# Filter chunks of a Hyena branch: one bank per parity of taps, wider steps, later matmuls, and another share for GpSimd

## The chip, the cores and the metric

The kernel runs on one core of a Trainium2 chip. The metric is device time in microseconds (us); of three runs the median counts. Engines are named as in the profile: PE (TensorE matmul), PEld (its weight loads), DVE (VectorE), ACT (ScalarE), POOL (GpSimd), SP (the queue that issues the DMAs).

## The reference

Two layers of an encoder trunk on x of 256 rows by 1024 columns, float32. Per layer:

```python
u = rms_norm(x, norm_mix_pre)
proj = u @ w_in                      # q, k, v of 3 groups x 4 heads, and hv, hx1, hx2
o_att = attention of the 3 dilated windows, mixed by their softmax denominators
filt = implicit_filters(...)         # a small MLP with sines -> 4 x 1024 channels x 256 taps, times a decay
z = hx1 * bidir_fft_conv(hv, filt[0], filt[1], hy_bias[0])
z = hx2 * bidir_fft_conv(z, filt[2], filt[3], hy_bias[1])
merged = sigmoid(u @ w_gate + b_gate) halves times (o_att @ w_o_attn, z @ w_o_hyena), summed
x = x + rms_norm(merged @ w_out, norm_mix_post)
x = x + rms_norm(swiglu(rms_norm(x, norm_ffn_pre)), norm_ffn_post)
```

The filters of a layer depend on its weights alone, not on x.

## The kernel before

**Precision.** Every big product is three matmuls (`mm3`): each float32 operand is split into a high and a low part, and high by high, high by low and low by high are summed. So each piece of weights (`raw`, 128 by 1024 or 128 by 768) is loaded by SP (L140), copied to `whi` by ACT (L86), and `wlo = raw - whi` is made by DVE or by POOL (L89). `split_lo` counts the pieces; each one whose count is a multiple of `POOL_LO` = 5 goes to POOL. A piece is split up to three pieces ahead of its use (`AHEAD`), and four raw buffers are in flight.

**Order of the work.** PE runs in the order in which the program writes its matmuls. The other engines' queues are put in order by a planner that simulates the program beforehand; the queues are then fixed and each engine works through its own strictly in order.

**Ticks.** Between two pieces of weights PE does a step of side work. Side jobs are Python generators in a queue; at most two are active; one `tick()` advances each active one to its next `yield`. So a `yield` more is a piece of weights (12 matmuls of 384 columns or 24 of 256) between two steps of a job. The jobs of the first layer's mixer, in queue order: two filter MLPs, constants, eight filter chunks (4 column groups `cc` times 2 convolutions `v`), attention slots 0 and 1, four jobs of two convolutions each (`both`), attention slots 2 and 3. Numbered from the mixer's start, the pieces are: slot 0 (pieces 1 to 4), slot 1 (5 to 16), the input columns of the Hyena branch (17 to 40), gates (41 to 56), slot 2 (57 to 68), slot 3 (69 to 80), the Hyena output projection (81 to 88). There is a tick after each. Before slot 3's values (piece 77) the program runs ticks until all four convolution jobs have ended, and then splits their result (`z_split`: `zh` on ACT, `zl` on DVE), which pieces 81 to 88 use.

**A filter chunk** (`filter_chunk`, one per `cc` and `v`) has three steps. *Load*: SP loads `w`, `dec` and `bb` (the bias row; one buffer only), POOL makes `sd` (sum and difference), ACT and DVE (POOL in layer 2) split it into `sh` and `sl`. *D*, two ticks later (four for the chunks with `cc == 2` of layer 2): for each parity `e` of taps two matmuls give `h`, DVE multiplies it by the decay in two 256-column instructions (`dd`, L315), ACT and DVE split it (`dh`, `dl`). *Z*, two ticks later: for each half `s` (cosine, sine) one PSUM bank takes both parities, 12 matmuls in all; then per `s` one 256-column `ev` (L332 on DVE, L334 on ACT) and two 256-column DVE instructions into the tables `K` (L337 to L341). Layer 1's eight chunks run in its mixer. Layer 2's first four run during layer 1's feed-forward part and its last four in layer 2's own mixer.

**Convolution and attention.** `conv` multiplies a transformed block `zz` by `K` (L562 to L564 on DVE, L565 and L566 on POOL). `attend` makes scores and a softmax (`S`, L634 to L639), yields three times, transposes the result on PE (L647, `PT`) and multiplies it by the values.

Of the kernel before, what the change touches and what calls it, by code (L numbers as in the profile page):

```python
# [44 lines left out]
def trunk(tc, nc, a, out):  # L45
# [4 lines left out]
    with es:  # L50
# [11 lines left out]
        def bigt(dt=F32, name="big"):  # L62
            return big.tile([P, 1024], dt, tag="big", bufs=22, name=name)
# [7 lines left out]
        def f256(name, dt=F32):  # L71
            return sm.tile([P, L], dt, tag="f256", bufs=4, name=name)
# [7 lines left out]
        def mm3(o, lh, ll, rh, rl, start, stop):  # L80
            mm(o, lh, rh, start, False)
            mm(o, lh, rl, False, False)
            mm(o, ll, rh, False, stop)
# [46 lines left out]

        source = order()
        loaded, halfway, ready = deque(), deque(), deque()
        shared = [True]
        count = [0, 0]

        def load(spare=False):
# [21 lines left out]
        def split_lo(eng=None):  # L158

            if halfway:  # L160
                raw, n, h, lo, own = halfway.popleft()
                count[1] += 1
                share = shared[0] and count[1] % POOL_LO == 0 or count[1] == 6
                lo_of(lo[:, :n], raw[:, :n], h[:, :n], nc.gpsimd if share else eng)
                ready.append((h, lo, own))

# [115 lines left out]
        def filter_chunk(l, v, cc, K, fd, shared):  # L282
            w = t512("w3")
            nc.sync.dma_start(w, a["w3"][l, v, cc])
            if v == 0:
                dec = sm.tile([P, 2, 256], F32, tag="dec", bufs=2, name="dec")
                nc.sync.dma_start(dec, a["dec"][cc])
                shared[cc] = dec
            dec = shared[cc]
            bb = sm.tile([P, 256], F32, tag="bb", bufs=1, name="bb")  # L290
            nc.sync.dma_start(bb, a["hyb"][l, v, cc * 256:(cc + 1) * 256].partition_broadcast(P))
            if cc % 2 == 0:
                for j in range(2):
                    K[v][j][cc // 2] = bigt(name=f"K{v}{j}{cc // 2}")
            sd = t512("sd")
            h = ptt(sd[:, 0:256], w[:, 0:256], w[:, 256:512], op=OP.add)
            late = l == 1 and cc == 2
            if late and v == 0:
                tc.keep_in_program_order(h)
            ptt(sd[:, 256:512], w[:, 0:256], w[:, 256:512], op=OP.subtract)  # L300
            sh, sl = r512("sh"), r512("sl")
            h = hi_of(sh, sd)
            if l == 0 and cc == 0:
                tc.keep_in_program_order(h)
            lo_of(sl, sd, sh, nc.gpsimd if l else None)
            for _ in range(4 if late else 2):
                yield
            Dh, Dl = [], []
            for e in range(2):
                h = acc()  # L310
                mm(h, gst[l][:, e, :], sh, True, False)
                mm(h, gst[l][:, e, :], sl, False, True)
                d = t512("dd")
                for q in range(2):
                    vtt(d[:, q * 256:(q + 1) * 256], h[:, q * 256:(q + 1) * 256], dec[:, e, :], op=OP.mult)  # L315
                dh, dl = r512("dh"), r512("dl")
                hi_of(dh, d)
                lo_of(dl, d, dh)
                Dh.append(dh)
                Dl.append(dl)  # L320
            yield
            yield
            hh, cq = cc // 2, cc % 2
            for s in range(2):
                z = acc()
                for e in range(2):
                    b = (2 * s + e) * P
                    mm3(z[:, e * 256:(e + 1) * 256], fd[:, b:b + P], fd[:, 512 + b:512 + b + P],
                        Dh[e][:, s * 256:(s + 1) * 256], Dl[e][:, s * 256:(s + 1) * 256], True, True)
                ev = f256("ev")  # L330
                if s == 0:
                    vtt(ev, z[:, 0:256], bb, op=OP.add)  # L332
                else:
                    nc.scalar.activation(ev, z[:, 0:256], AF.Copy)  # L334
                k0 = K[v][0][hh][:, cq * 512 + s * 256: cq * 512 + s * 256 + 256]
                k1 = K[v][1][hh][:, cq * 512 + s * 256: cq * 512 + s * 256 + 256]
                vtt(k0, z[:, 256:512], ev, op=OP.add)  # L337
                if s == 0:
                    vtt(k1, ev, z[:, 256:512], op=OP.subtract)
                else:  # L340
                    vtt(k1, z[:, 256:512], ev, op=OP.subtract)  # L341
            yield


# [193 lines left out]
        def conv(v, cc, z, xg, K):  # L538

            f, b = fold(z)  # L540
            eo = sm.tile([P, 2, 2, P], F32, tag="t512", bufs=7, name="eo")
            ptt(eo[:, 0].rearrange("p c (r a) -> p c r a", r=4), f, b, op=OP.add)
            ptt(eo[:, 1].rearrange("p c (r a) -> p c r a", r=4), f, b, op=OP.subtract)
            yield
            yield
            t = acc()
            for q in range(4):
                nc.tensor.transpose(t[:, q * P:(q + 1) * P], eo[:, q // 2, q % 2, :], ident)  # L548
            nh, nl = r512("nh"), r512("nl")
            hi_of(nh, t)  # L550
            lo_of(nl, t, nh)
            yield
            yield
            Y = []
            for j in range(2):
                zz = acc()
                for s in range(2):
                    mm3(zz[:, s * 256:(s + 1) * 256], dft_h[:, 2 * s + j, :], dft_l[:, 2 * s + j, :],
                        nh[:, s * 256:(s + 1) * 256], nl[:, s * 256:(s + 1) * 256], True, True)
                Kt = K[v][j][cc // 2][:, (cc % 2) * 512:(cc % 2) * 512 + 512]  # L560
                t1, t2 = t512("t1"), t512("t2")
                vtt(t1, zz, Kt, op=OP.mult)  # L562
                vtt(t2[:, 0:256], zz[:, 0:256], Kt[:, 256:512], op=OP.mult)
                vtt(t2[:, 256:512], zz[:, 256:512], Kt[:, 0:256], op=OP.mult)  # L564
                ptt(t1[:, 0:256], t1[:, 0:256], t1[:, 256:512], op=OP.subtract)  # L565
                ptt(t1[:, 256:512], t2[:, 0:256], t2[:, 256:512], op=OP.add)  # L566
                Y.append(t1)
            yield
            yield
            pq = acc()  # L570
            for c in range(2):
                for s in range(2):
                    w = slice(s * 256 + c * P, s * 256 + (c + 1) * P)
                    for j in range(2):
                        mm(pq[:, w], Y[j][:, w], inv[:, 2 * s + j, :], j == 0, j == 1)
            pe = f256("pe")
            nc.scalar.activation(pe, pq[:, 0:256], AF.Copy)
            ys = t512("ys")
            vtt(ys[:, 0:256], pq[:, 256:512], pe, op=OP.add)
            vtt(ys[:, 256:512], pe, pq[:, 256:512], op=OP.subtract)  # L580
            f, b = fold(xg)
            for q, w in enumerate((f, b)):
                ptt(w, w, ys[:, q * 256:(q + 1) * 256].rearrange("p (c r a) -> p c r a", c=2, r=4), op=OP.mult)
            yield
            yield
# [23 lines left out]
        def attend(s, qk, vt, OT):  # L609
# [16 lines left out]
            for i in range(2):  # L626
# [10 lines left out]
                nc.scalar.activation(Si, Si, AF.Exp, bias=nm, scale=SCALE, accum_out=den)  # L637
                nc.vector.reciprocal(rd, den)
                nc.vector.tensor_scalar(Si, Si, rd, None, op0=OP.mult)  # L639
            yield  # L640
            yield
            yield
            PT = bigt(name="PT")
            for i in range(2):
                t = acc()
# [27 lines left out]
        def mixer(l, U, o, K):  # L673
# [6 lines left out]
            def slot(s, qk, then=None):  # L680
                vt = bigt(name="vt")
                for j in range(3) if s else (2,):
                    if j == 2 and then:
                        while convs[0]:
                            tick()
                        then()
                    o = [acc() for i in range(2)]
                    for kk in range(4):
                        pc = piece()
                        for i in range(2):  # L690
                            rows_of(U, o[i], i, pc, kk, 384)
                        done(pc)
                        if kk < 3:
                            tick()
                    for i in range(2):
                        qkv_out(j, i, o[i], qk, vt)
                    tick()
                return attend(s, qk, vt, OT)

            queue.append(slot(0, qk))  # L700
            queue.append(slot(1, [bigt(name="qk") for i in range(2)]))

# [3 lines left out]
            for cc in range(4):  # L706
# [13 lines left out]

                queue.append(both())

            GT = [bigt(name="GT") for h in range(4)]
            for c in range(16):
                nc.scalar.activation(ct(GT, c), col_proj(U), AF.Sigmoid, bias=bgt[:, l, c:c + 1])
# [234 lines left out]
```

## Time and profile before

| | before |
|---|---|
| median of 3 runs (lowest, highest) | 1107.41 us (1107.06, 1108.79) |
| profiled execution, its own time | 1109.53 us |
| its span | 1107.6 us |
| granted PE clock, mean | 0.996 |
| PE busy | 1083.8 us (98%), 7624 matmuls |
| DVE / ACT / POOL busy | 709.9 (64%) / 557.1 (50%) / 396.9 us (36%) |
| HBM | 184.89 MB read, 168 GB/s |

The span is what the instructions take up; the profiled execution's own time is 1.9 us more than it and 2.1 us more than the median of the three runs. A busy PE is not a PE at its peak: the rows' times of its matmuls overlap. Idle time on any engine but PE costs nothing here unless PE waits for it.

### The profile page before, as it was taken

The page shows a single profiled execution, that of the slowest core. Times are in us where ns is not written, and L with a number is a line of the kernel's source. Part 1 is how long each engine was busy: PE and PEld are TensorE (multiplying, and loading weights), DVE is VectorE, ACT ScalarE, POOL GpSimd, SP SyncE. Part 2 cuts the span into 40 slices and gives each one's busy share as a digit, 9 for nine tenths or more (in the row PEclk, how much of TensorE's full clock was granted, in tenths as well). Part 3 has the DMA queues.
Part 4 walks back from the last instruction along what each step waited for, and adds up shares of the span by engine and source line. Part 5 has one row for each costly group of instructions (what it writes and reads, how often), then busy time and mean ns, then how long its engine had stood idle before and what let it go on. Part 6 is the DMA issues. An engine that isn't in the chain of part 4 may idle for free.

```text
span 1107.6 us, 19530 instructions
## 1 busy us (share of the span) xinstructions
PE 1083.8 (98%) x7624; PEld 1039.0 (94%) x7624; DVE 709.9 (64%) x1139; ACT 557.1 (50%) x852; POOL 396.9 (36%) x488
## 2 busy tenths in 40 slices
PE   8989999999999999999999999999999999999997
PEld 6989999999899899998879899999999989999986
DVE  5799985556647756665474877865545586554554
ACT  6555564443545645454464564454356455544442
POOL 2643133468614134211115714455645230111110
PEclk9999999999999999999999999999999999999999
DMA  8565544434446555656655454444355475465662
GB/s 295 174 211 193 159 138 134 133 117 128 148 143 201 186 188 185 192 182 223 193 169 165 144 166 134 136 151 131 122 162 196 149 232 190 151 183 182 197 199 79
DMA packets 59878, 187.21 MB, mean 169 GB/s; under 512 B 6919, under 2 KB 9353, under 8 KB 59786
## 3 DMA queue, kind: packets, MB, share of 16 engines
q1 hardware_dynamic: 59786, 185.96, 52.6%
q8 instruction: 60, 0.98, 0.4%
q14 instruction: 32, 0.26, 0.1%
HBM read 184.89 MB, written 1.05 MB: 168 GB/s over the span
## 4 chain that ended last, share of the span: by engine, by line
PE 87%; DVE 6%; DMA 3%; ACT 2%; issue 1%; POOL 1%; SPq 0%; DVEq 0%; POOLq 0%; ACTq 0%
PE acc L78 84%; DVE wlo L89 2%; PE acc L617 1%; DVE dl L89 1%; ACT whi L86 1%; DVE dd L315 1%; DMA mask<-in_mask_dram 1%; DMA raw<-in_wq_dram 1%; ACT jk L352 1%; DMA raw<-in_wa_dram 1%; PE acc L647 1%; PE acc L548 1%; PE acc L397 1%; DVE arg L241 0%; DMA w<-in_w_dram 0%
## 5 line engine op out<-in xcount | busy, mean ns | idle before, releaser
L86 ACT ACTIVATE whi<-raw 128x1024 fp32r<-128x1024 f32 (+1 forms) x352 | 345.4, 989 | 384.5 <-PE acc L78 292.6
L89 DVE TENSOR_TENSOR wlo<-raw,whi 128x1024 fp32r<-128x1024 f32 (+1 forms) x294 | 346.4, 1186 | 231.7 <-ACT whi L86 229.2
L78 PE MATMUL acc<-UH,whi 128*128 128x256 f32 x1248 | 356.0, 285 | 0.0
L78 PE MATMUL acc<-UH,wlo 128*128 128x256 f32 x1248 | 353.1, 283 | 0.0
L78 PE MATMUL acc<-UL,whi 128*128 128x256 f32 x1248 | 353.0, 283 | 0.0
L89 POOL TENSOR_TENSOR wlo<-raw,whi 128x1024 fp32r<-128x1024 f32 (+1 forms) x58 | 133.3, 2298 | 412.1 <-ACT whi L86 412.0
L78 PEld LDWEIGHTS acc<-UL,whi 128*128 128x128 f32 x1248 | 239.3, 192 | 0.4
L78 PEld LDWEIGHTS acc<-UH,whi 128*128 128x128 f32 x1248 | 239.2, 192 | 0.4
L78 PEld LDWEIGHTS acc<-UH,wlo 128*128 128x128 f32 x1248 | 239.2, 192 | 0.0
L78 PE MATMUL acc<-wlo,UH 128*128 128x384 f32 x448 | 152.4, 340 | 2.4 <-DVE wlo L89 1.3
L78 PE MATMUL acc<-whi,UH 128*128 128x384 f32 x448 | 153.8, 343 | 0.0
L78 PE MATMUL acc<-whi,UL 128*128 128x384 f32 x448 | 151.1, 337 | 0.0
L78 PE MATMUL acc<-whi,hs 128*128 128x512 f32 x352 | 108.9, 389 | 0.0
L78 PEld LDWEIGHTS acc<-wlo,UH 128*128 128x128 f32 x448 | 85.3, 190 | 5.7 <-DVE wlo L89 4.1
L78 PEld LDWEIGHTS acc<-whi,UH 128*128 128x128 f32 x448 | 85.5, 191 | 1.3 <-ACT whi L86 0.4
L78 PEld LDWEIGHTS acc<-whi,UL 128*128 128x128 f32 x448 | 85.1, 190 | 0.2 <-DVE UL L89 0.2
L78 PEld LDWEIGHTS acc<-whi,hs 128*128 128x128 f32 x352 | 66.1, 188 | 13.6
L78 PE MATMUL acc<-wlo,hs 128*128 128x512 f32 x176 | 68.6, 390 | 0.5 <-DVE wlo L89 0.5
L799 DVE TENSOR_TENSOR HF<-acc,silu 128x256 f32<-128x256 f32 x38 | 16.1, 424 | 49.1 <-PE acc L78 49.1
L359 POOL TENSOR_SCALAR nv<-ss 128x1 f32<-128x1 f32 x16 | 7.0, 440 | 103.7 <-ACT jk L352 103.7
L78 PEld LDWEIGHTS acc<-wlo,hs 128*128 128x128 f32 x176 | 33.0, 188 | 7.7 <-DVE wlo L89 0.9
L89 DVE TENSOR_TENSOR hs<-HF,hs 128x256 fp32r<-128x256 f32 x44 | 31.1, 724 | 10.3 <-ACT hs L86 10.3
(165 smaller groups left out, 1678.9 us busy)
## 6 DMA issues: line engine op xcount, KB each, us to landing
raw<-in_wa_dram SPq DMA_DIRECT2D x240, 512.0 KB, 3.6
raw<-in_wq_dram SPq DMA_DIRECT2D x96, 384.0 KB, 3.2
raw<-in_wg_dram SPq DMA_DIRECT2D x16, 384.0 KB, 3.8
w<-in_w_dram SPq DMA_DIRECT2D x16, 256.0 KB, 4.3
gain<-in_gains_dram SPq DMA_DIRECT2D x7, 512.0 KB, 6.2
dec<-in_dec_dram SPq DMA_DIRECT2D x8, 256.0 KB, 3.8
bb<-in_hyb_dram SPq DMA_DIRECT2D x16, 128.0 KB, 4.0
dftraw<-in_dft_dram SPq DMA_DIRECT2D x3, 256.0 KB, 4.4
```

The costliest lines, as they stand in the source:

```text
L78: nc.tensor.matmul(o, lT, r, start=start, stop=stop)
L86: return nc.scalar.activation(o, i, AF.Copy)
L89: (eng or nc.vector).tensor_tensor(o, i, h, op=OP.subtract)
L315: vtt(d[:, q * 256:(q + 1) * 256], h[:, q * 256:(q + 1) * 256], dec[:, e, :], op=OP.mult)
L352: nc.scalar.activation(jk, half, AF.Square, scale=D ** -0.5, accum_out=ss[:, h:h + 1])
L359: nc.gpsimd.tensor_scalar(v, ss[:, 0:1], ss[:, 1:2], EPS, op0=OP.add, op1=OP.add)
L397: nc.tensor.transpose(t[:, q * P:(q + 1) * P], u[:, h * 512 + q * P: h * 512 + (q + 1) * P], ident)
L548: nc.tensor.transpose(t[:, q * P:(q + 1) * P], eo[:, q // 2, q % 2, :], ident)
L617: nc.tensor.transpose(t[:, q * P:(q + 1) * P], qk[i][:, j * 384 + g * P: j * 384 + (g + 1) * P], ident)
L647: nc.tensor.transpose(t[:, q * P:(q + 1) * P], S[:, i * 512 + q * P:i * 512 + (q + 1) * P], ident)
L799: vtt(ct(HF, f), ob, sl, op=OP.mult)
```

## The change

A filter chunk's Z step takes a PSUM bank per parity of taps instead of one per half `s`; the same 12 matmuls run in another order (`e` outside, `s` inside). `dd` becomes one 512-column instruction, with `dec` broadcast. The even bank is copied whole by ACT into `ev` (512 columns), POOL adds the bias row to its first half, and two 512-column DVE instructions make `K`. The sine half of `K`'s second table has the other sign for it, which `conv` takes up by swapping an addition and a subtraction; its two 256-column products become one of 512 columns that reads `K`'s halves in reverse order. The ticks between D and Z become three in layer 1, four for the `cc == 2` chunks of layer 2, and stay two for its others. Attention slot 2 yields five times instead of three between its softmax and the transposes. And from the mixer's start to the end of its input columns, in layer 1 alone, POOL takes each third piece instead of each fifth.

```diff
@@ -130,7 +130,7 @@
-        shared = [True]
+        shared = [True, POOL_LO]
@@ -160,7 +160,7 @@
-                share = shared[0] and count[1] % POOL_LO == 0 or count[1] == 6
+                share = shared[0] and count[1] % shared[1] == 0 or count[1] == 6
@@ -311,34 +311,31 @@
                 d = t512("dd")
-                for q in range(2):
-                    vtt(d[:, q * 256:(q + 1) * 256], h[:, q * 256:(q + 1) * 256], dec[:, e, :], op=OP.mult)
+                vtt(d[:, :].rearrange("p (q c) -> p q c", q=2), h[:, :].rearrange("p (q c) -> p q c", q=2),
+                    dec[:, e:e + 1, :].to_broadcast([P, 2, 256]), op=OP.mult)
...
-            yield
-            yield
-            hh, cq = cc // 2, cc % 2
-            for s in range(2):
+            for _ in range(4 if late else 2 if l else 3):
+                yield
+
+            Z = []
+            for e in range(2):
                 z = acc()
-                for e in range(2):
-                    b = (2 * s + e) * P
-                    mm3(z[:, e * 256:(e + 1) * 256], fd[:, b:b + P], fd[:, 512 + b:512 + b + P],
-                        Dh[e][:, s * 256:(s + 1) * 256], Dl[e][:, s * 256:(s + 1) * 256], True, True)
-                ev = f256("ev")
-                if s == 0:
-                    vtt(ev, z[:, 0:256], bb, op=OP.add)
-                else:
-                    nc.scalar.activation(ev, z[:, 0:256], AF.Copy)
-                k0 = K[v][0][hh][:, cq * 512 + s * 256: cq * 512 + s * 256 + 256]
-                k1 = K[v][1][hh][:, cq * 512 + s * 256: cq * 512 + s * 256 + 256]
-                vtt(k0, z[:, 256:512], ev, op=OP.add)
-                if s == 0:
-                    vtt(k1, ev, z[:, 256:512], op=OP.subtract)
-                else:
-                    vtt(k1, z[:, 256:512], ev, op=OP.subtract)
+                for s in range(2):
+                    b, w = (2 * s + e) * P, slice(s * 256, (s + 1) * 256)
+                    mm3(z[:, w], fd[:, b:b + P], fd[:, 512 + b:512 + b + P], Dh[e][:, w], Dl[e][:, w], True, True)
+                if e == 0:
+                    ev = t512("ev")
+                    nc.scalar.activation(ev, z, AF.Copy)
+                    ptt(ev[:, 0:256], ev[:, 0:256], bb, op=OP.add)
+                Z.append(z)
+
+            w = slice((cc % 2) * 512, (cc % 2) * 512 + 512)
+            vtt(K[v][0][cc // 2][:, w], Z[1], ev, op=OP.add)
+            vtt(K[v][1][cc // 2][:, w], ev, Z[1], op=OP.subtract)
             yield
@@ -560,10 +557,13 @@
                 vtt(t1, zz, Kt, op=OP.mult)
-                vtt(t2[:, 0:256], zz[:, 0:256], Kt[:, 256:512], op=OP.mult)
-                vtt(t2[:, 256:512], zz[:, 256:512], Kt[:, 0:256], op=OP.mult)
-                ptt(t1[:, 0:256], t1[:, 0:256], t1[:, 256:512], op=OP.subtract)
-                ptt(t1[:, 256:512], t2[:, 0:256], t2[:, 256:512], op=OP.add)
+                zv, kv, tv = (x.rearrange("p (s c) -> p s c", s=2) for x in (zz[:, :], Kt, t2[:, :]))
+                vtt(tv, zv, kv[:, ::-1, :], op=OP.mult)
+                ptt(t1[:, 0:256], t1[:, 0:256], t1[:, 256:512], op=OP.add if j else OP.subtract)
+                if j:
+                    ptt(t1[:, 256:512], t2[:, 256:512], t2[:, 0:256], op=OP.subtract)
+                else:
+                    ptt(t1[:, 256:512], t2[:, 0:256], t2[:, 256:512], op=OP.add)
@@ -637,9 +637,8 @@
-            yield
-            yield
-            yield
+            for _ in range(5 if s == 2 else 3):
+                yield
@@ -697,6 +696,7 @@
+            shared[1] = POOL_LO if l else 3
             queue.append(slot(0, qk))
@@ -720,6 +720,7 @@
+            shared[1] = POOL_LO
             GT = [bigt(name="GT") for h in range(4)]
```

## Rows read from the trace of the kernel before

**Rows 1.** The page, busy time of each engine, its share of the span and its instructions.

```profile
PE 1083.8 (98%) x7624; PEld 1039.0 (94%) x7624; DVE 709.9 (64%) x1139; ACT 557.1 (50%) x852; POOL 396.9 (36%) x488
```

**Rows 2.** What PE waited for over the span: who waited, for whom, us in total, times, the longest.

```profile
PE acc L78 <- DVE dl L89: 7.4, 6, 2.3
PE acc L647 <- DVE S L639: 2.4, 1, 2.4
...
PE acc L78 <- DVE wlo L89: 1.8, 5, 0.5
...
PE acc L78 <- POOL sl L89: 0.8, 1, 0.8
```

**Rows 3.** Four stretches: start and end, length, then busy us and instructions of PE, PEld, DVE, ACT and POOL, the granted PE clock, the DMA share and GB/s.

```profile
55.00:64.00 9.00, 5.99 (x33) 5.34 (x33) 8.94 (x17) 5.55 (x11) 4.64 (x8) 0.97 0.66 223
...
104.00:114.00 10.00, 8.03 (x65) 7.63 (x64) 10.00 (x22) 5.16 (x9) 5.20 (x5) 1.00 0.73 237
...
280.00:312.00 32.00, 29.62 (x194) 29.21 (x192) 16.62 (x23) 17.79 (x28) 16.51 (x32) 0.95 0.47 149
...
600.00:614.00 14.00, 10.75 (x62) 9.38 (x61) 10.75 (x18) 7.90 (x13) 8.64 (x8) 1.00 0.35 108
```

**Rows 4.** Short stretches behind two of PE's waits, the same columns.

```profile
63.50:66.90 3.40, 3.40 (x14) 3.40 (x14) 3.40 (x8) 0.38 (x1) 3.40 (x6) 0.50 0.99 316
66.90:70.30 3.40, 3.40 (x25) 3.40 (x25) 1.84 (x4) 2.24 (x4) 3.40 (x6) 1.00 0.37 137
302.85:305.90 3.05, 3.05 (x11) 3.05 (x12) 1.59 (x2) 0.60 (x2) 0.00 (x0) 0.51 0.73 230
```

**Rows 5.** PE's timeline from 306 us, two pairs of successive matmuls of 384 and of 256 columns: start, duration, instruction.

```profile
306.11 0.33 PE L78 MATMUL acc<-whi,UL 128*128 128x384 f32 x1
306.28 0.33 PE L78 MATMUL acc<-whi,UH 128*128 128x384 f32 x1
...
308.82 0.28 PE L78 MATMUL acc<-zh,wlo 128*128 128x256 f32 x1
308.94 0.28 PE L78 MATMUL acc<-zh,whi 128*128 128x256 f32 x1
```

**Rows 6.** Timelines of POOL (first row) and DVE from 54 to 64 us, around the first chunk's Z step.

```profile
54.28 2.57 POOL L89 TENSOR_TENSOR wlo<-raw,whi 128x768 fp32r<-128x768 f32 x1
...
55.06 1.94 DVE L242 TENSOR_SCALAR arg<-arg 128x256 f32<-128x256 f32 x1
...
60.29 1.41 DVE L315 TENSOR_TENSOR dd<-acc,dec 128x256 f32<-128x256 f32 x4
...
62.48 1.47 DVE L89 TENSOR_TENSOR dl<-dd,dh 128x512 fp32r<-128x512 f32 x2
```

**Rows 7.** Timelines of DVE and POOL from 102 to 106 us.

```profile
102.82 3.49 DVE L89 TENSOR_TENSOR dl<-dd,dh 128x512 fp32r<-128x512 f32 x2
...
103.14 2.62 POOL L89 TENSOR_TENSOR wlo<-raw,whi 128x1024 fp32r<-128x1024 f32 x1 [12.65 <-ACT whi L86]
```

**Rows 8.** POOL's timeline at 300 us, and one row of the view of tile `S`: duration in ns, least, median and most, of its 16 instructions (the longest one started at 300.72 us), first and last start.

```profile
299.87 2.55 POOL L89 TENSOR_TENSOR wlo<-raw,whi 128x1024 fp32r<-128x1024 f32 x1 [0.73 <-ACT whi L86]
...
L639 DVE TENSOR_SCALAR S<-S,rd x16: 476/482/1985, 152.0 to 865.5; 128x512 f32<-128x512 f32 x16
```

**Rows 9.** DVE's timeline from 604 to 614 us (layer 2's `cc == 2` chunks).

```profile
607.71 2.97 DVE L89 TENSOR_TENSOR dl<-dd,dh 128x512 fp32r<-128x512 f32 x3
```

**Rows 10.** Groups of instructions by line and shape on POOL, ACT and DVE: count, busy us, mean ns of one, idle time before.

```profile
L89 POOL TENSOR_TENSOR wlo<-raw,whi 128x1024 fp32r<-128x1024 f32 x43 | 103.8, 2413 | 394.8 <-ACT whi L86 394.7
...
L565 POOL TENSOR_TENSOR t<-t 128x256 f32<-128x256 f32 x32 | 23.4, 736 | 38.9 <-DVE t L562 37.9
...
L620 ACT ACTIVATE G<-acc 128x512 f32<-128x512 f32 x16 | 8.6, 588 | 1.0 <-PE acc L617 0.8 <-PE acc L78 0.2
...
L89 DVE TENSOR_TENSOR wlo<-raw,whi 128x1024 fp32r<-128x1024 f32 x197 | 247.9, 1264 | 154.5 <-ACT whi L86 152.1 <-issue 2.0
```

**Rows 11.** DVE's timeline from 72 and from 186 us: starts that follow each other without a gap.

```profile
72.55 0.41 DVE L337 TENSOR_TENSOR K<-acc,ev 128x256 f32<-128x256 f32 x1
72.89 0.41 DVE L339 TENSOR_TENSOR K<-ev,acc 128x256 f32<-128x256 f32 x1
...
186.10 0.69 DVE L562 TENSOR_TENSOR t<-acc,K 128x512 f32<-128x512 f32 x1 [1.52 <-PE acc L78]
186.71 0.42 DVE L563 TENSOR_TENSOR t<-acc,K 128x256 f32<-128x256 f32 x1
```

**Rows 12.** A stretch with the instructions on `wlo` alone: length, busy us and count of PE, PEld, DVE and POOL, clock, DMA.

```profile
29.00:172.00 143.00, 75.81 (x256) 48.81 (x255) 35.72 (x31) 19.07 (x8) 0.99 0.53 170
```

**Rows 13.** The stretch of layer 1's filter chunks, all instructions, columns as in rows 3.

```profile
55.00:140.00 85.00, 80.02 (x592) 77.92 (x592) 81.65 (x174) 47.65 (x76) 26.84 (x29) 0.98 0.58 188
```

**Rows 14.** Timelines of PE, POOL and ACT around the last convolution of layer 1.

```profile
280.38 1.95 PE L78 MATMUL acc<-inv,t 128*128 128x128 f32 x16
...
284.53 1.43 POOL L583 TENSOR_TENSOR X<-X,ys 128x256 f32<-128x256 f32 x2
...
293.16 2.00 ACT L86 ACTIVATE zh<-X 128x1024 fp32r<-128x1024 f32 x2
```

**Rows 15.** What SP's queue waited for.

```profile
SPq L140 <- POOL wlo L89: 198.4, 54, 11.5
...
SPq L291 <- DVE ev L332: 19.2, 14, 4.0
```

## The prediction

> **What bounds the kernel now.** I read the page first: PE is busy 98% of the span [rows 1], so the matmuls set the time and only what makes PE stand still can be won. The change keeps their number and shapes (12 per Z step, as before), so I asked next what PE waits for. The view of waits is short [rows 2]: 7.4 us in six waits for `dl` (the low part that a Z step needs), 2.4 us in one wait for `S` (attention), 0.8 us for `sl`, and 1.8 us in five waits for `wlo`, none over 0.5 us. So the pieces of weights are split early enough, and the side work is not.
>
> The stretches say where [rows 3]: PE idles 9.00 - 5.99 = 3.0 us at 55 to 64 us and 10.00 - 8.03 = 2.0 us at 104 to 114 us (`dl` of layer 1), 32.00 - 29.62 = 2.4 us at 280 to 312 us (`S`, attention slot 2 of layer 1), and 14.00 - 10.75 = 3.2 us at 600 to 614 us, 0.8 of it `sl` and 2.4 `dl` of layer 2's first late chunks. The `dl` parts add up to the 7.4 us of the waits.
>
> Two of these cost more than they show. Behind the first, PE's granted clock is 0.50 (the 1.2 GHz level) from 63.5 to 66.9 us, and it made 14 matmuls in 3.4 us where the next 3.4 us at 1.00 hold 25: (25 - 14) / 25 x 3.4 = 1.5 us lost. Behind the wait for `S` the clock is 0.51 and seven 384-column and four small matmuls took 3.05 us; at the full clock's 0.17 us each [rows 5] the seven take 1.2 us, and with some 0.5 us for the others about 1.3 us are lost [rows 4]. Before both, PE had stood for over 2 us at one place. The other two left the clock at 1.00 [rows 3].
>
> So the stalls that the change touches are worth 3.0 + 2.0 + 2.4 + 2.4 = 9.8 us idle and 1.5 + 1.3 = 2.8 us of half clock: 12.6 us.
>
> Why is `dl` late? DVE is busy 81.65 of 85 us in layer 1's chunk stretch [rows 13], and part of that is standing. A `dl` takes 0.7 us, but a pair took 3.49 us while POOL made a `wlo` from 103.14 to 105.76 us, and ended 0.55 us behind it [rows 7]; `arg` took 1.94 us in the same way and ended just behind POOL's 54.28 to 56.85 us [rows 6]; and the `S` of the wait took 1.99 us instead of 0.48, with a `wlo` on POOL until 302.42 us [rows 8]. DVE instructions with all operands in SBUF stand while POOL works there.
>
> The Trainium skill says why (SBUF — State Buffer, Who interferes with whom): DVE and GpSimd share one pair of SBUF ports, an exclusive lock for a whole instruction, and a DVE instruction with two SBUF inputs or in a two-port mode blocks behind GpSimd. The three rows above agree. The rule speaks against the part of the change that gives POOL more pieces; what that would do is the second rival below.
>
> **The change part by part.** *More ticks between D and Z, layer 1.* One piece more lies between them: 12 x 0.17 = 2.1 us in slot 1, 24 x 0.12 = 2.9 us in the columns [rows 5]. At 104 to 114 us the two waits sum to 2.0 us: gone. At 55 to 64 us the sum is 3.0 us against 2.1 us, but DVE also reaches the second `dl` sooner: POOL's piece at 54.28 us, which held `arg` for 1.6 us, falls elsewhere with another count, and two `dd` groups get shorter. The new order needs the odd `dl` only after six matmuls, the old one after three, 0.4 us. I take 0.7 us as left (0 if all of this holds, 3.0 - 2.1 = 0.9 if only the tick counts, 2.4 if a POOL piece lands there again and holds a `dl` for 1.5 us). With under 1 us of standing I expect no half clock: its 1.5 us goes too.
>
> *Four ticks, layer 2's late chunks.* Two pieces of 2.1 us against 2.4 us of waits; there too POOL's `sd` held the `dl` (three in 2.97 us, about 1 us each [rows 9]). Gone. The 0.8 us for `sl` lies before D and stays.
>
> *Five yields in slot 2.* The transposes move two pieces later, into the output projection with 24 matmuls each: 5.8 us more against 2.4 us. Gone, with its 1.3 us of clock.
>
> *What the extra ticks push.* Layer 1's eight chunks run two at a time, six ticks a pair before, seven now: everything behind them moves by 4 ticks. Counting the yields through the queue, the last convolution job ended two ticks before slot 3's values; now the loop that waits for the jobs runs two ticks with no piece between. These issue only slot 2's first transposes, so PE has no hole of itself. But the last inverse matmuls now come four pieces ahead of the use of their result instead of eight. The last inverse matmuls ended at 282.33 us and POOL had gated the result at 285.96 us, 3.6 us later [rows 14]; `zh` of a tile is 1.0 us and `zl`, a DVE instruction of the same size as a `wlo`, 1.3 us [rows 10, 14]: 6 us, and some 2 more if a `wlo` of POOL's gets in between. Four pieces of 2.1 us and slot 2's small matmuls give 8.4 to 11 us. Cost 0; 3 us if the planner puts POOL's rotary work and a piece ahead of it.
>
> *DVE's instructions.* Successive 256-column ones follow at 0.33 us, a 512-column one takes 0.61 [rows 11]. Per chunk `dd` falls from 4 x 0.33 to 2 x 0.61 and `ev` and `K` from 5 x 0.33 to 2 x 0.61: 2.97 to 2.44, so 0.5 us, 4 us over layer 1's chunks. In `conv` 2 x 0.33 becomes 0.61, nothing. PE doesn't see this but through `dl`. Reading through a broadcast or a reversed half isn't in the trace; at worst each of the 8 x 2 broadcasts costs as the two instructions that it replaces.
>
> *The bias on POOL.* `ev` is now a 512-column ACT copy (0.59 us by the copy of `G`) and then a POOL addition (0.74 us by L565), and DVE's two `K` instructions wait for it [rows 10]. That is a new wait at the head of DVE's queue: `wlo`, `dl` and `dd` of the next chunk stand behind it, and PE behind these. It is free when the planner puts `K` late enough, since `K` is first read by the convolutions, at 186 us [rows 11]. With a 2.41 us `wlo` ahead on POOL it is up to 3.2 us a chunk. `bb` has one buffer, so its next load on SP now waits for POOL: SP stood 19.2 us there before, 4.0 at most, with raw loads behind [rows 15], and no piece was late by over 0.5 us [rows 2]. I take 0.
>
> *A third of the pieces on POOL.* From the mixer's start, 39 pieces were split on DVE (31) and POOL (8) [rows 12]; a third is 13 or 14, so six move. DVE saves 6 x 1.2 us and may be held once for each. A hold ran from 0 to 2.2 us [rows 7]; in the stretch with chunks two of POOL's pieces stand ahead of idle time of PE (3.0 and 2.0 us) [rows 3, 6, 7]. With a tick more of cover than the longest hold, I take six holds at 0.2 us = 1.2 us (0 to 6 x 1.5 = 9). SP's raw loads wait for POOL to free a buffer, 11.5 us at the longest [rows 15], and that too has stayed off PE.
>
> *Sum.* -12.6 + 0.7 (first Z step) + 1.2 (holds) + 0.5 (new small waits: a changed planner's order has seldom none) = -10.2 us. The profiled execution would go from 1109.5 to 1099.3 us; the median of the runs is 2.1 us under it, so **1097.2 us**.
>
> **The rivals.** *The stall moves on.* DVE has 3.35 us free in the 85 us of the chunk stretch [rows 13]. If it is full, a tick more only lets it fall behind a tick later, or the planner puts `wlo` ahead of `dl` since it sees more time, so the change doesn't do what it says. For it: the busy share; against it: much of that is standing, and the work gets some 9 us shorter. Layer 1's 5.0 + 1.5 us stay, 2.4 + 1.3 + 2.4 = 6.1 us are won: 1101.3 us.
>
> *POOL's pieces hold DVE.* Six more pieces and eight bias additions on POOL in a stretch full of SBUF instructions of DVE. If each of the six costs PE 1.0 us, as the two did on average at the old cover after the saved `wlo` (5.0 / 2 less 1.2), what layer 1's chunks win goes: -12.6 + 6.5 + 6 = about 0, 1107 us. The point is whether a hold of up to 2.2 us is longer than the tick of 2.1 to 2.9 us. Against it: in the rows the longest one is not, and not each piece of POOL's meets an instruction that PE is about to need. (It is what the rule from the Trainium skill above would come to here.)
>
> *DVE stands at `K`, slower than before.* Place: layer 1's chunks, DVE's queue behind POOL's bias addition. Price: up to 8 x 3.2 = 25 us, less the room on DVE (3.35 us free, 4 us from wider steps, some 5 us of moved pieces, about 12): 13 us on PE; layer 1's `dl` gains gone, 6.1 us won elsewhere: +7, 1114 us. It decides from 12 / 8 = 1.5 us of standing per chunk. For it: a fixed order and a POOL piece that takes twice DVE's; against it: POOL is busy 27 of 85 us there [rows 13].
>
> **How the numbers follow.** A run of this kernel can be told from no change at about 0.2%, 2.2 us. Forecast 0.55 (1093 to 1100.5); the stall moves on 0.23 (1100 to 1105); holds 0.12 (1104 to 1110); `K` 0.10 (1109 to 1117). Faster: all of the first two and a sixth of the third, 0.80; the same: most of the third, 0.10; slower: 0.10. The low end is everything won and the `sl` wait and half of the `wlo` waits besides (12.6 + 0.8 + 0.9 = 14.3): 1093.1. Above, I leave out the last rival and part of the holds: 1107.5. Range 1093.0 to 1107.5.
>
> **What would show it.** In the changed kernel's waits, `dl` under 1.5 us and no `S`; PE's clock at 1.00 after 64 and 303 us; `sl` still there at 602 us. The stall moved on: `dl` or `wlo` waits of 4 us or more before 140 us. Holds: DVE's `dl` or `wlo` of over 1.5 us ending with POOL's `wlo`, and PE waiting right then. `K`: idle DVE before L337's successor put down to POOL `ev`. A wait of PE for `zl` near 300 us would mean that the four pushed ticks were not free. A span that falls by under 2 us makes the forecast wrong.

## The result and the profile after

The changed kernel took 1120.36 us (median of 4 runs, 1119.18 to 1121.38) where the kernel before took 1107.24 beside it: the ratio is 1.0111, 95% interval 1.0095 to 1.0128. The medians differ by 13.1 us, the ratio comes to 12.3; 1097.2 was forecast, and the time lies outside the range of 1093.0 to 1107.5. All ratios are of runs in the chip's faster state; the medians of `a_evbb_nothird` and `a_w_bbf` below count one slow run each, and are 1111.97 and 1103.15 us without it. The profiled execution took 1120.36 us, its span is 1118.6.

The page's busy times [rows 1]: DVE has less to do, POOL more, and PE's share has fallen.

```profile
PE 1086.6 (97%) x7624; PEld 1040.8 (93%) x7624; DVE 698.6 (62%) x1022; ACT 559.8 (50%) x852; POOL 424.3 (38%) x509
```

What PE waited for, of which the first three rows are new in size [rows 2]:

```profile
PE acc L78 <- POOL sl L89: 7.6, 3, 5.2
PE acc L78 <- DVE sl L89: 4.7, 3, 2.4
PE acc L78 <- ACT sh L86: 4.1, 2, 2.9
...
PE acc L78 <- DVE G L622: 1.6, 1, 1.6
...
PE acc L78 <- POOL t L564: 0.8, 2, 0.6
PE acc L78 <- POOL t L566: 0.2, 1, 0.2
```

The waits that the change aimed at are gone: no row for `dl` and none for `S`. In their place PE stands 16.4 us for `sl` and `sh`, the two inputs of the D step, one step earlier in the chunk. Stretches around the three places, with start and end, length, busy us of PE, PEld, DVE, ACT and POOL, the granted clock, DMA share and GB/s:

```profile
73.60:76.50 2.90, 0.30 (x3) 0.10 (x1) 1.74 (x3) 0.37 (x1) 2.49 (x4) 1.00 0.78 269
76.50:83.30 6.80, 4.09 (x13) 3.30 (x14) 6.80 (x7) 2.73 (x6) 5.70 (x3) 0.50 0.49 149
...
134.50:138.00 3.50, 3.09 (x11) 2.81 (x12) 3.00 (x6) 1.15 (x2) 1.62 (x2) 0.51 0.46 150
...
629.50:639.70 10.20, 5.16 (x15) 4.87 (x16) 8.21 (x8) 2.42 (x4) 6.42 (x9) 0.50 0.40 125
```

Behind the stands the clock is at half (the 1.2 GHz level) in three stretches instead of two [rows 4]. The account of the two profiled executions, 1120.36 - 1109.53 = 10.8 us: waits for `sl`, `sh`, `G` and `t` of 16.4 + 1.6 + 1.0 = 19.0 against 7.4 + 2.4 + 0.8 = 10.6 for `dl`, `S` and `sl` before, +8.4; PE's busy time at half clock 4.09 + 3.09 + 5.16 = 12.3 against 3.40 + 3.05 = 6.5, and half of the difference (what the lower clock takes) is +2.9. Together 11.3, about what was measured.

**Why `sl` is late.** The chain of waits of the changed kernel from 64 to 82 us, in order of time (start, us, what):

```profile
68.10 0.70 POOL ev L333
...
68.82 5.06 DMA bb<-in_hyb_dram
...
74.01 0.73 POOL ev L333
...
75.37 0.68 DVE K L338
76.05 0.81 DVE wlo L89
...
77.10 2.85 DVE sl L89
...
80.00 2.08 PE acc L78 x5
```

GpSimd's first bias addition frees the one `bb` buffer, the next bias takes 5.06 us to land, and GpSimd stands for it with the next chunk's `sd` behind. From there the chain goes through DVE: `K` waits for that `ev`, a `wlo` follows, and the `sl` behind it takes 2.85 us beside a `wlo` of GpSimd's (last section), where one in `a_w` without such company took 0.68. Most of the 2.4 us that PE stood for this `sl` is that hold. That is one chain. The other is in SP's queue (start, duration, line). The kernel before:

```profile
59.60 0.43 SPq L284 DMA_DIRECT2D w<-in_w_dram  x1
...
62.96 0.43 SPq L284 DMA_DIRECT2D w<-in_w_dram  x1
...
65.97 4.26 SPq L291 DMA_DIRECT2D bb<-in_hyb_dram  x2
```

and the changed one:

```profile
68.82 0.33 SPq L291 DMA_DIRECT2D bb<-in_hyb_dram  x1
69.19 1.29 SPq L284 DMA_DIRECT2D w<-in_w_dram  x1
...
71.64 0.43 SPq L284 DMA_DIRECT2D w<-in_w_dram  x1
```

Before, both `w` of the next chunks go out ahead of the load of `bb`; after, they stand behind it, 9 us later, and so does all that is made of them. The changed `ev` is a `t512` tile, as `w` is, where the old one was an `f256` tile. Two more rows of the changed kernel's waits, on POOL and on DVE:

```profile
DVE K L337 <- POOL ev L333: 21.9, 11, 3.5
POOL ev L333 <- DMA bb<-in_hyb_dram: 14.8, 5, 5.2
```

The theories: **W**, `ev` among the seven `t512` buffers makes the next chunk's `w` late; **B**, GpSimd stands at its bias addition behind the one `bb` buffer; **P**, GpSimd's third of the pieces is in the way; **T**, added later, the ticks themselves start the next chunk's load too near to its D step.

### The profile page after: what moved, and what is told of

It reads as the page before. It is cut to its first block, busy times and chain, and to the rows that moved or that the text cites. A ratio compares the mean times of both kernels' runs of the same rounds, so it can differ in the third digit from the quotient of the medians.

```text
span 1118.6 us, 19467 instructions
## 1 busy us (share of the span) xinstructions
PE 1086.6 (97%) x7624; PEld 1040.8 (93%) x7624; DVE 698.6 (62%) x1022; ACT 559.8 (50%) x852; POOL 424.3 (38%) x509
## 4 chain that ended last, share of the span: by engine, by line
PE 85%; POOL 5%; DVE 4%; DMA 2%; ACT 2%; issue 2%; POOLq 0%; DVEq 0%; SPq 0%; ACTq 0%
PE acc L78 82%; DVE wlo L89 1%; DMA bb<-in_hyb_dram 1%; ACT whi L86 1%; POOL wlo L89 1%; PE acc L617 1%; PE acc L394 1%; DMA w<-in_w_dram 1%; ACT jk L349 1%; PE acc L545 1%; PE acc L646 1%; DVE sl L89 1%; DMA raw<-in_wa_dram 0%; POOL ev L333 0%; DVE arg L241 0%
## 5 line engine op out<-in xcount | busy, mean ns | idle before, releaser
L89 POOL TENSOR_TENSOR wlo<-raw,whi 128x1024 fp32r<-128x1024 f32 (+1 forms) x63 | 145.3, 2306 | 375.5 <-ACT whi L86 365.4
L89 DVE TENSOR_TENSOR hs<-HF,hs 128x256 fp32r<-128x256 f32 x44 | 34.3, 799 | 10.0 <-ACT hs L86 10.0
```

The costliest lines, as they stand in the source:

```text
L89: (eng or nc.vector).tensor_tensor(o, i, h, op=OP.subtract)
```

## The experiments

Letters: `a_` is the changed kernel with one edit or a few, `b_` the kernel before with one or two. All ratios are to the kernel before, with the 95% interval.

**First four: one suspect each.** `b_ev512` gives the kernel before nothing but `ev`'s new group of buffers:

```diff
-                ev = f256("ev")
+                ev = sm.tile([P, L], F32, tag="t512", bufs=7, name="ev")
```

> The kernel before, with nothing changed but that its 256-column `ev` takes its buffers from the group of `w`, `sd` and `dd`. Theory W: the next chunk's `w` falls behind `ev` on SP's queue, PE waits for `sl` or `sh` by 4 us or more, time 1111 to 1120 us. Theories B and P: as before, 1106 to 1109 us, since the additions stay on DVE and the pieces are shared as before.

1117.9 us, ratio 1.0094 [1.0066, 1.0122]. No instruction differs, and a loss nearly as large as the change's is there. Its queue shows the changed kernel's order in layer 1, and in layer 2 two `w` some 12 to 13 us later than the kernel before, which sends them out at 604.67 and 606.87 us (SP, as above):

```profile
66.31 0.33 SPq L291 DMA_DIRECT2D bb<-in_hyb_dram  x1
66.69 0.42 SPq L284 DMA_DIRECT2D w<-in_w_dram  x1
...
616.49 0.43 SPq L284 DMA_DIRECT2D w<-in_w_dram  x1
...
620.27 0.58 SPq L284 DMA_DIRECT2D w<-in_w_dram  x1
```

What PE waited for:

```profile
PE acc L78 <- DVE dl L89: 8.5, 6, 2.3
PE acc L78 <- POOL sl L89: 3.3, 2, 2.4
```

The time is where theory W put it, but the loss is not the same one. The 3.3 us for `sl` (4 or more were expected) all lie in layer 2, and from 600 to 640 us the granted clock is 0.91 on average, where it was 1.00. In layer 1 PE still stands for `dl` (6.5 us from 55 to 140 us, 5.0 in the kernel before) and not for `sl`. So late `w` loads cost time by themselves; the 16.4 us of the changed kernel take its other parts too.

`a_ev` takes `ev` out of that group in the changed kernel, into the five buffers that the feed-forward uses for `hs`:

```diff
-                    ev = t512("ev")
+                    ev = sm.tile([P, 512], F32, tag="hs", bufs=5, name="ev")
```

> The changed kernel, with `ev` alone moved to another group of buffers (that of `hs`, idle in the chunks' time). Theory W (slots are given out in program order, so an `ev` in the group of `w` pushes the next chunk's `w` load behind the Z step): the `w` loads come ahead of the Z steps again, PE's waits for `sl` and `sh` fall from 16.4 us to under 3, time 1097 to 1102 us. Theory B (POOL's bias addition stands for the single `bb` buffer and `sd` stands behind it): the waits stay over 10 us, time 1113 us or more. Theory P (POOL's third of the pieces): unchanged, 1118 to 1122 us.

1112.22 us, ratio 1.0036 [1.0024, 1.0048]: some two thirds of the loss gone, and layer 2's two `w` out at 604.54 and 606.60 us again. But 9.6 us of PE waits are left, 7.6 for `sl` and `sh` and 2.0 for `dl`, where theory W expected under 3 us for `sl` and `sh` and at most 1102 us: W is not the whole. `a_bb` gives `bb` the tag `hs` in the same way, and `a_nothird` leaves GpSimd every fifth piece:

```diff
-            shared[1] = POOL_LO if l else 3
+            shared[1] = POOL_LO
```

> The changed kernel, with `bb` alone given more buffers. Theory B: POOL's additions no longer stand for `bb` (14.8 us before), `sd` comes in time, time 1098 to 1104 us. Theory W: `w` still comes behind the Z step; part of the waits stays, time 1110 us or more. Theory P: 1118 to 1122 us.

> The changed kernel, with POOL on each fifth piece throughout. Theory P: most of the loss goes, time 1107 us or less. Theories W and B: the waits for `sl` and `sh` stay over 10 us, 1115 to 1122 us.

`a_bb`: 1117.58 us, 1.0085 [1.0063, 1.0107]. `a_nothird`: 1117.51 us, 1.0081 [1.0063, 1.0099]. Each is some 0.3% better than the changed kernel (quotient of the ratios), with 12.7 and 13.0 us of `sl` and `sh` waits still there: neither B nor P carries the loss by itself. In `a_bb` five `bb` are out by 25 us and the two `w` still go at 69.71 and 71.04 us, so it is not a `bb` waiting ahead of them in SP's queue that holds them back.

**Second four: what is left when `ev` is out.**

```diff
# b_ticks: the kernel before, with the change's ticks alone
-            yield
-            yield
+            for _ in range(4 if late else 2 if l else 3):
+                yield
...
-            yield
-            yield
-            yield
+            for _ in range(5 if s == 2 else 3):
+                yield
# a_evbb: ev and bb both in hs; a_evbb_nothird: and every fifth piece
# a_dveadd: the changed kernel, bias addition on VectorE
-                    ptt(ev[:, 0:256], ev[:, 0:256], bb, op=OP.add)
+                    vtt(ev[:, 0:256], ev[:, 0:256], bb, op=OP.add)
```

> The kernel before with the later steps alone: three, four and two ticks between D and Z, five yields in slot 2; banks, widths, `ev`, bias and shares as before. Theories W and B (the loss is in `ev`'s buffers and in the bias on POOL): `dl` and `S` go as forecast and no wait for `sl` or `sh` over 1.5 us comes, 1096 to 1101 us. Theory T (the ticks themselves push the next chunk's load too close to its D step): waits for `sl` and `sh` of 5 us or more, 1104 us or more.

> The changed kernel with both `ev` and `bb` in the other group of buffers. If W and B together are the cause: waits for `sl` and `sh` under 3 us in all, 1098 to 1104 us. If the ticks are (T): the waits stay as with `ev` alone (7.6 us), 1109 us or more.

> The changed kernel with the bias addition on DVE instead of POOL; `ev` and `bb` as changed. Theory B: POOL no longer stands for `bb`, `sd` is only as late as its `w`; half of the waits for `sl` and `sh` go, 1109 to 1114 us. Theory W alone: 1116 us or more.

> As the run with both `ev` and `bb` moved, and POOL on each fifth piece throughout. Theory P (the third costs): 1 us or more faster than that run. Otherwise within 1 us of it, or slower by the 4 to 5 us of work that goes back to DVE.

`b_ticks`: 1112.01 us, 1.0018 [1.0003, 1.0033]. The ticks were to carry the whole gain, and by themselves they win nothing. PE no longer stands for `S`, and for `dl` 3.6 us instead of 7.4, but there are 6.0 us for `sl` and `sh`, where there were 0.8: theory T's signs, and neither W's nor B's. SP's queue says why: one `w` now goes out behind two biases. The kernel before, then `b_ticks`:

```profile
79.29 0.42 SPq L284 DMA_DIRECT2D w<-in_w_dram  x1
...
81.95 0.43 SPq L284 DMA_DIRECT2D w<-in_w_dram  x1
```

```profile
80.63 0.43 SPq L284 DMA_DIRECT2D w<-in_w_dram  x1
...
91.15 0.33 SPq L291 DMA_DIRECT2D bb<-in_hyb_dram  x1
...
96.33 0.33 SPq L291 DMA_DIRECT2D bb<-in_hyb_dram  x1
...
97.84 0.42 SPq L284 DMA_DIRECT2D w<-in_w_dram  x1
```

`a_evbb`: 1110.55 us, 1.0006 [0.9989, 1.0023]. `a_dveadd`: 1123.6 us, 1.0133 [1.0099, 1.0167]: the addition is no better on VectorE, so it is not GpSimd as such. `a_evbb_nothird`: 1113.07 us, 1.0027 [1.0007, 1.0047]: with `ev` and `bb` moved, leaving out the third gains nothing (the two intervals overlap), so P falls. `a_evbb` keeps 6.5 us of `sl` waits and, as T expected, does not come under 1109.

**Third: take `w` itself out of `t512`.** If the late load is the cause, in T as in W, this should mend both kernels; the third run is the control.

```diff
# a_w: the changed kernel; b_ticks_w: b_ticks; b_w: the kernel before
-            w = t512("w3")
+            w = sm.tile([P, 512], F32, tag="hs", bufs=5, name="w3")
```

> The changed kernel, with one edit: the weight tile `w` of a filter chunk is taken from the five 512-wide buffers of the feed-forward's `hs` instead of the seven of `t512`. Theory: the changed kernel is slow because the chunk's `w` has to wait its turn in `t512` behind other tiles, is loaded some 10 us too late, and the D step then stands for `sl` and `sh` (16.4 us of waits). Then the loads of the second and third chunk go out before the Z step of the first again, the waits for `sl` and `sh` fall from 16.4 us to under 5, and the time is 1098 to 1106. Rival one, it is `ev` that must leave `t512` (1112 with that alone, measured), because `dd`, `sd` and the convolution's tiles stand behind it: then `w` alone gives no more than that, 1112 to 1117. Rival two, the third tick between D and Z of layer 1 in itself is what starts the next chunk late: then the time stays at 1115 to 1120, with the same waits.

> The kernel before, with the additional ticks alone (3, 4 and 2 between D and Z; 5 in the attention of slot 2) and `w` in the buffers of `hs`. With the ticks alone the time was 1112.0 against 1109.9, because one `w` went out 16 us later than in the kernel before and its D step stood 4 us at `sl`. If that load is late for want of a buffer of `t512`, the waits for `sl` and `sh` (6 us) go, the `dl` waits of layer 1 (7 us before) stay gone or small, and the time is 1099 to 1106. If the ticks in themselves make it late, the time stays at 1110 to 1113.

> The control: the kernel before, with `w` in the buffers of `hs` and nothing else. Its loads were in time already; what it stands at is `dl` and `S` (12.6 us). So all theories expect 1105 to 1111, within 0.3% of the kernel before. If it is faster by more, the gain of the other two kernels with this edit is not from the ticks or the wide steps, but from `w`'s buffers alone.

`a_w`: 1106.3 us, 0.9962 [0.9948, 0.9975]. `b_ticks_w`: 1105.71 us, 0.9953 [0.9936, 0.9970]. `b_w`: 1108.38 us, 0.9986 [0.9974, 0.9998]. One line takes 1.5% off the changed kernel (1.0111 to 0.9962, some 16 us), turns the ticks from a loss into a gain, and gives the kernel before little. In `a_w` seven `w` are out by 31 us, where every kernel with `w` in `t512` had two:

```profile
18.48 0.43 SPq L284 DMA_DIRECT2D w<-in_w_dram  x1
...
21.30 1.53 SPq L284 DMA_DIRECT2D w<-in_w_dram  x2
...
24.35 1.32 SPq L284 DMA_DIRECT2D w<-in_w_dram  x2
...
27.03 0.33 SPq L284 DMA_DIRECT2D w<-in_w_dram  x1
...
30.58 0.33 SPq L284 DMA_DIRECT2D w<-in_w_dram  x1
```

and of PE's waits for `sl`, `sh` and `dl` there remain

```profile
PE acc L78 <- DVE sl L89: 3.1, 2, 1.6
...
PE acc L78 <- DVE dl L89: 1.2, 1, 1.2
```

`b_w` is not a neutral control, though. From 600 to 640 us, where the kernel before idles 3.2 us, PE is busy throughout without a tick more (columns as above); in exchange it stands 3.1 us for `h`, ahead of the chunks:

```profile
600.00:640.00 40.00, 40.00 (x254) 39.23 (x253) 30.18 (x56) 23.94 (x38) 23.72 (x35) 1.00 0.48 152
```

**Last five: what the new Z step still costs.** `a_w_dveadd` is `a_w` with the addition on VectorE; `a_w_zold` is `a_w` with the Z step, and the convolution's signs, of the kernel before. The other three move buffers of `a_w` alone:

```diff
# a_w_evr
+                    ev = sm.tile([P, 512], F32, tag="r512", bufs=8, name="ev")
# a_w_bbf
+            bb = f256("bb")
# a_w_evr_bbf: both
```

> The changed kernel with `w` in the buffers of `hs`, and the addition of the bias `bb` on VectorE instead of GpSimd. With `w` moved alone the time was 1106.3; its chain from 95 to 135 us has the load of `bb` (GpSimd stands 8.3 us for it between 60 and 140 us, with the next chunk's `sd` queued behind) and two `sl` waits of PE (3.1 us). Theory B: what is left of the loss lies at GpSimd's queue behind `bb`; then these `sl` waits go and the time falls to 1102 to 1105. Rival: on VectorE the addition stands at the same load with the split pieces and `dl` behind it, as in the changed kernel, where the same edit cost 0.2%: 1106 to 1110.

> The changed kernel with `w` in the buffers of `hs`, and with the Z step of the kernel before (a bank per pair of frequency halves, four additions of 256 columns on VectorE, `ev` in `f256`) and the convolution's signs that belong to it. What is left of the change: the ticks, GpSimd's third, the wide `dd` and the wide `t2` products. Theory: the wide Z step is worth nothing by itself and costs the wait at `bb` on GpSimd; then this kernel is at least as fast as the kernel before with the ticks and `w` moved (1105.7): 1101 to 1106, with no `sl` waits on PE. Rival: the wide Z step is worth its 2 us of VectorE time: then this one is slower than the changed kernel with `w` moved (1106.3), 1107 to 1110.

> The changed kernel with `w` in the buffers of `hs` (1106.3) and `ev` in those of `r512` besides. The kernel with the old Z step and the rest of the change took 1103.0. If what the new Z step still costs is `ev`'s place among the `t512` buffers (the next chunk's `sd` and `dd` behind it), the two `sl` waits of PE (3.1 us) go and the time is 1101 to 1104. If it is the wait for `bb` at the head of GpSimd's queue, the waits stay and the time is 1105 to 1108.

> The changed kernel with `w` in the buffers of `hs` (1106.3) and `bb` in the four 256-wide buffers of `f256` instead of its single one, so that its load can go out ahead of the bias addition before it. If what is left of the loss is GpSimd standing for `bb`, GpSimd's wait for that load goes and the time is 1101 to 1104. If it is `ev`'s buffers, the time stays at 1105 to 1108. Both in part: 1103 to 1106 in each of the two.

> The changed kernel with all three: `w` in `hs`, `ev` in `r512`, `bb` in `f256`; the instructions are those of the changed kernel. If the late loads and the buffers were all that was wrong with the forecast, this one comes out as forecast or near it, 1097 to 1102, with under 2 us of PE waits for `sl` and `dl` together. If the wide Z step in itself (ScalarE copy, GpSimd addition, then the two sums) is late, it stays at 1104 to 1108, over the 1103.0 of the old Z step.

`a_w_dveadd`: 1110.45 us, 1.0011 [0.9994, 1.0027], worse than `a_w`. `a_w_zold`: 1103.03 us, 0.9939 [0.9918, 0.9960]. `a_w_evr`: 1105.66 us, 0.9970 [0.9957, 0.9983]; `a_w_bbf`: 1103.29 us, 0.9949 [0.9933, 0.9966]; `a_w_evr_bbf`: 1102.44 us, 0.9949 [0.9930, 0.9967]. Once `w` is in time no effect of `ev`'s place can be seen. The one `bb` buffer seems to cost 0.1 to 0.2%, within the intervals; in `a_w_bbf` the row of POOL's wait for `bb` is gone. The old and the new Z step cannot be told apart here. `a_w` and `a_w_evr_bbf` came out 0.3 and 0.4 us above what was expected if the late loads, or all the buffers, were the whole cause. Differences of this size may also come from the planner, which makes a new order for every version; no run separates the two. These last versions, `a_w_zold`, `a_w_bbf` and `a_w_evr_bbf`, beat both kernels: by 0.5 to 0.6% the kernel before, and by 1.6 to 1.7% the changed one (the quotient of the ratios).

## Why the prediction was wrong

**The step that failed** is "*The bias on POOL* ... I take 0", and with it "*What the extra ticks push* ... Cost 0". Of the new `ev` I counted the instructions, the engine and the wait, and not the group of buffers that it is allocated from. `b_ev512` shows that this alone costs 0.94%, some 10 us where I took 0: the next chunk's `w`, from the same group, goes out behind the Z step instead of ahead of it. In the changed kernel, where `dl` is in time, D then stands for `sl` and `sh`. Of the ticks I counted what they push at the end of the mixer, and not that they push the next chunk's `w` too: `b_ticks` at 1.0018 against `b_ticks_w` at 0.9953 is 7 us for that, of which `b_w` gains 1.5 without the ticks. With all of these buffers moved (`a_w_evr_bbf`, 0.9949) 1.6% of the changed kernel's time goes, some 18 of the 23 us between forecast and result. Why the planner puts these loads later is argued, not shown: the likely reason is that the buffers of a group are given out in the program's order, so that `w` cannot come ahead of an earlier tile of its group. A plain want of an eighth buffer would do the same, and `hs` gives `w` five buffers besides another group; no run separates these.

**The ceiling** was right as far as it goes. With `w`, `ev` and `bb` in other buffers and every instruction of the change kept (`a_w_evr_bbf`), the stretches that were to gain do (second and third row):

```profile
44.20:51.00 6.80, 6.80 (x21) 6.15 (x22) 4.42 (x11) 1.62 (x3) 0.70 (x1) 0.53 0.39 120
...
55.00:140.00 85.00, 84.15 (x630) 82.18 (x629) 79.68 (x138) 52.23 (x81) 47.29 (x49) 1.00 0.61 194
600.00:640.00 40.00, 40.00 (x273) 39.65 (x272) 27.21 (x39) 24.48 (x38) 22.11 (x34) 1.00 0.51 166
```

PE idles 0.85 us from 55 to 140 us where it idled 85.00 - 80.02 = 5.0 [rows 13], and nothing from 600 to 640 us, all at full clock. The second of these is not shown to be the change's: `b_w` has it too. That this kernel is still at 1102 and not at 1097 fits waits at places the forecast did not have:

```profile
PE acc L78 <- DVE wlo L89: 2.5, 5, 0.9
...
PE acc L78 <- ACT h L243: 2.1, 1, 2.1
PE acc L78 <- DVE G L622: 1.6, 1, 1.6
...
PE acc L78 <- DVE sl L89: 0.9, 2, 0.7
PE acc L78 <- POOL t L564: 0.8, 2, 0.6
```

The wait for `h` at 42 us, in the filter network ahead of the chunks, is new and leaves the clock at 0.53 until 51 us (first row of the stretches); `b_w` has it too (3.1 us), so it belongs to moving `w` and not to the change. A likely reason is that `w`'s loads now crowd the start: the chain to that `h` begins with a load of `raw` of 7.17 us, where the page's median is 3.2. The `G` wait is in `b_ticks` as well: it comes with the ticks or the five yields, which no run separates. "New small waits" were put at 0.5 us; `G` and `t` alone are 2.4, and the five waits for `wlo` have grown from 1.8 [rows 2] to 2.5.

**The parts.** *Ticks*: `dl` and `S` went, as forecast. *Five yields*: right about `S`; no wait for `zl` came near 300 us. *DVE's instructions*: right, also for the broadcast and the reversed half that the trace of before could not show (grouped by line and shape: count, busy us, mean ns, idle before):

```profile
L561 DVE TENSOR_TENSOR t<-acc,K 128x512 f32<-128x512 f32 x32 | 21.7, 679 | 0.3 <-POOL t L566 0.3
L314 DVE TENSOR_TENSOR dd<-acc,dec 128x512 f32<-128x512 f32 x32 | 20.9, 683 | 3.3 <-PE acc L78 3.3
```

679 and 683 ns are what the plain 512-column product took, 0.69 us [rows 11]; but DVE was not what bound. *The third*: the pieces moved and cost nothing that could be seen, as `a_evbb` against its version without the third shows. *Late chunks*: the four ticks did not keep layer 2's places free; 7.6 us of `sl` waits came there, and went with `w`'s move.

**The rivals.** "DVE stands at `K`" had the sign, the place and nearly the time (1114), with a chance of 0.10. Its rows came, 21.9 us of DVE standing for POOL's `ev`. But its mechanism, DVE's queue held long enough to make PE late, is not what decides, though `K` is a link of the chain shown above: `a_w` keeps the order copy, GpSimd addition, `K`, and 15.9 us of that standing, and is faster than the kernel before. The waits were to be for `dl` and `wlo` in DVE's queue; they were for `sl` and `sh`, whose weights had been loaded late. "The stall moves on" had the better picture, PE standing one step on, without seeing that the move could cost more than the stall. "POOL's pieces hold DVE" falls as the main cause by the two runs without the third, though single holds are there, one of them in that chain. (Its working has a slip: 5.0 / 2 less 1.2 is 1.3 us a piece and not 1.0, which makes its time about 1109.)

## What to carry to other kernels

A change of a tile's tag is a change of the schedule: when an edit widens a tile or gives it another group of buffers, list what else that group holds, and ask whose load will now go out later. When steps are pushed apart, look at the next turn's first load as well as at this turn's consumer, and read it from the DMA queue's order, since waits downstream name an engine (`sl` on DVE or POOL) and not the load. When a change loses, put each buffer back by itself before an instruction is blamed: here one line that changes no instruction was worth 1.5%.

## What the runs showed of the hardware that I had not expected

The half clock lasted longer where PE stood again. In the changed kernel the half clock held for 3.5 us from 134.5 us, behind stands of PE; but for 6.8 us from 76.5 us and for 10.2 us from 629.5 us, where PE, already at half, stood another 2.4 and 5.2 us (it was busy 4.09 and 5.16 us of the two stretches). Before, it held some 3 us each time [rows 4]. In the three stretches PE's 12.3 busy us did the work of some 6, which the sum of the waits does not show. The length of one stand does not settle it: for `h`, PE stood 2.1 us in `a_w_evr_bbf` and the clock was at 0.53 behind it, 2.5 us in `a_w_evr` and the clock stayed at 1.00 from 40 to 60 us.

GpSimd and VectorE were both slow when they ran together. On the changed kernel's timelines around 77 us, POOL's row and two of DVE's:

```profile
76.05 3.34 POOL L89 TENSOR_TENSOR wlo<-raw,whi 128x1024 fp32r<-128x1024 f32 x1
```

```profile
75.97 1.22 DVE L89 TENSOR_TENSOR wlo<-raw,whi 128x1024 fp32r<-128x1024 f32 x1
77.10 2.84 DVE L89 TENSOR_TENSOR sl<-sd,sh 128x512 fp32r<-128x512 f32 x1
```

An `sl` without such company took 0.68 us (at 100.93 us in `a_w`), and POOL's `wlo` of this size takes 2.41 on average [rows 10]. By the lock that the Trainium skill describes (SBUF — State Buffer, Who interferes with whom) the `sl` would wait until POOL's instruction is over; it ended 0.5 us after it, and the trace agrees. That POOL's own instruction grows by 0.9 us in such company was new to me. DVE's `wlo` had begun just before it and ran for some 1.1 us of it; whether POOL stood for that one is not shown.
